# Splitting 32 weight units ahead of time: the attention's weights are split during the first MLP and parked in DRAM as two parts

## The chip, the cores and the metric

The kernel runs on one core of a Trainium2 chip, alone, as one program. The metric is the device time of that program in microseconds; several executions are timed and the median is given. The engines named here are TensorE (PE, with its weight loads PEld), VectorE (DVE), ScalarE (ACT), GpSimd (POOL) and SyncE (SP, which only issues DMAs). Line numbers such as L190 are lines of the kernel before; lines of the changed kernel are some 30 to 36 higher.

## The reference

A two-layer decoder trunk on 512 tokens of width 1024, with 16 learned meta tokens in front (528 columns in all), in float32:

```python
h = concat(meta, x)
# layer 0: mLSTM heads beside an RG-LRU branch, one output projection
h = h + ab_mixer(rmsnorm(h, norm_mix[0]))
h = h + mlp(rmsnorm(h, norm_mlp[0]), w1[0], w2[0])
# layer 1: differential attention, 8 heads, q/k of 2 x 64, v of 128, partial rotary
q, k, v = split(rmsnorm(h, norm_mix[1]) @ c_w_in)
p = softmax(q0 k0^T) - lam * softmax(q1 k1^T)      # causal, per head
h = h + (rmsnorm(p @ v) * subln * (1 - lambda_init)) @ c_w_out
h = h + mlp(rmsnorm(h, norm_mlp[1]), w1[1], w2[1])
out = rmsnorm(h, norm_final)[16:]
# mlp(x, w1, w2) = square(relu(x @ w1)) @ w2, hidden width 4096
```

## The kernel before

**Units.** All large weights lie in DRAM as 225 units `wu[u]` of 128 x 1024 float32 (512 KB). The list `seq` gives the order in which they are used: places 65 to 128 are the first MLP, 129 to 152 the attention's q, k and v projections (three units for each of 8 heads), 153 to 160 the attention's output projection, 161 to 224 the second MLP.

**Two parts.** A product in near float32 precision is made of three passes on rounded operands: each operand is split into a high part, rounded to the type `fp32r`, and a low part, the rest. `emit_load` does this for a unit: SP loads it into `raw` (two buffers), ACT casts it into `wh` (L159) and DVE subtracts, `wl = raw - wh` (L115, the helper `sub`). For the places listed in `POOL_L` the subtraction is done by POOL. `wh` and `wl` have three buffers each, so a part of unit i can be written only when the matmuls of unit i-3 are done. `get_w` sees to it that the load of unit i+2 is written down when unit i is used.

**A unit's matmuls.** `unit_mm` (L190) runs 8 blocks of the contraction times 3 passes, on 528 columns in two halves of 264 (48 matmuls) or on 512 columns (24 matmuls). Results lie in four PSUM buffers `mm`; a unit of two halves takes two of them, so PE can run one unit ahead of the engine that reads the results.

**The first MLP** (`mlp`) goes through four quarters `q`. In each, eight units give `a0` to `a7`: DVE scales and clips the PSUM result into `rt` (L662), ACT squares it (L664) and splits it, ACT the high and DVE the low part (`a7h`, `a7l`). Eight more units `c` multiply these and DVE adds the results onto `h` (L673). At the end `norm_x` turns `h` into the split operand `dx` of the next layer; the squares `nsq` are added up by POOL (L243) for the root-mean-square `drstd`.

**The attention.** `attend(hd)` runs the three projections of a head. The rotary part goes over ACT (`qr`), DVE (`qs`, a shuffle, then a product with the table `tb`), POOL (`qr * tb`), DVE (sum, split into `rh` and `rl`), and SP DMAs that lay the halves out as `st` and `kz`. In between stand the steps of the heads before (`slot`, `SLOTS`): scores `psc`, their maximum (DVE, L810), exponentials `e` (ACT, L817), the combination of the two softmaxes (DVE, L827), its transposes `pt` (PE, L838), the split `pp`, and the product `po`.

**Order.** The program is recorded in the order of the Python code and a scheduler of the framework then sets each engine's own order, by priorities (`soon()`, `pri()`) and by its own model of durations. On the chip each engine takes its instructions strictly in that order and waits in front of the first that is not ready; so an instruction that waits holds up all behind it on its engine.

Of the kernel before, what the change touches and what calls it, by code (L numbers as in the profile page):

```python
# [10 lines left out]
F32 = mybir.dt.float32  # L11
F32R = mybir.dt.float32r
# [4 lines left out]
P = 128  # L17
# [20 lines left out]
U_MLP0 = 65  # L38
# [14 lines left out]

POOL_OPS = "Mm"

POOL_L = {5, 33, 43, 44, 52, 126, 140, 143, 149, 151, 155, 159, 161, 164}
N_S = 31

N_KZ = 3
LOAD1 = 9  # L60
# [4 lines left out]
C_NMIX0, C_NMIX1, C_NMLP0, C_NMLP1, C_NFIN, C_MN, C_CW, C_CB, C_BR, C_BI, C_LAM, C_SUB, C_IB, C_FB = (  # L65
    0, 8, 16, 24, 32, 40, 48, 80, 88, 96, 104, 112, 113, 114)
# [3 lines left out]
def unit_of(t):  # L70
    a = [int(c) for c in t[1:]]
    if t[0] == "q":
        return U_HEAD + 6 * a[0] + a[1]
    if t[0] == "e":
        return U_GATE
    if t[0] == "o":
        return U_O + a[0]
    return U_LRU + 4 * (a[0] // 2) + a[0] % 2 + (2 if t[0] == "g" else 0)


def trunk(tc, hT, wu, wri, pk, lv, rope, gf, out, probe=None):
    nc = tc.nc
# [6 lines left out]
    with ctx:  # L89
        cp = ctx.enter_context(tc.tile_pool(name="cp", bufs=1))  # L90
        wr = ctx.enter_context(tc.tile_pool(name="wr", bufs=2))
        wp = ctx.enter_context(tc.tile_pool(name="wp", bufs=3))
# [3 lines left out]
        dr = ctx.enter_context(tc.tile_pool(name="dr", bufs=1, space=bass.MemoryType.DRAM))  # L96
# [7 lines left out]
        def sc(name, dt=F32, w=T):  # L104

            return big.tile([P, T], dt, tag="s", name=name, bufs=N_S)

# [6 lines left out]
        def sub(eng, o, a, b):  # L114
            eng.tensor_tensor(out=o, in0=a, in1=b, op=ALU.subtract)  # L115

        def split(hl, src, sl=slice(0, T), eng=None):
            nc.scalar.copy(hl[0][:, sl], src)  # L118
            sub(eng or nc.vector, hl[1][:, sl], src, hl[0][:, sl].bitcast(F32))
# [15 lines left out]
        def soon():  # L135
            return tc.high_priority(offset=BOOST)
# [4 lines left out]

        seq = list(range(N_UNIT))
        ready = []
        seq[0:U_OUT0] = [unit_of(t) for t in PLAN if t[0] in "qeocg"]
        seq[U_OUT0:U_OUT0 + 16] = [U_OUT0 + (8 + i) % 16 for i in range(16)]
        state = {"next": 0, "use": 0}

        def emit_load():
            i = state["next"]
            u = seq[i]  # L150
            raw = wr.tile([P, 1024], F32, tag="raw", name=f"raw{i}")
            nc.sync.dma_start(out=raw, in_=wu[u])
            if u >= N_UNIT - 8:
                wh, wl = (wp.tile([P, 1024], F32R, tag="wf" + p, name=f"w{p}{i}", bufs=8) for p in "hl")
            else:
                wh = wp.tile([P, 1024], F32R, tag="wh", name=f"wh{i}")
                wl = None if u == U_GATE else wp.tile([P, 1024], F32R, tag="wl", name=f"wl{i}")
            with soon():
                nc.scalar.copy(wh, raw)  # L159
                eng = nc.gpsimd if i in POOL_L else nc.vector  # L160
                if u == U_GATE:

                    hi, r = (a.rearrange("p (k c) -> p k c", k=KB) for a in (wh, raw))
                    sub(eng, hi[:, :, 64:100], r[:, :, 0:36], hi[:, :, 0:36].bitcast(F32))
                else:
                    sub(eng, wl, raw, wh.bitcast(F32))
            ready.append((wh, wl))
            state["next"] += 1

        def get_w(u):  # L170
            while state["next"] <= min(state["use"] + 2, len(seq) - 1):
                emit_load()
            assert seq[state["use"]] == u
            state["use"] += 1
            return ready.pop(0)
# [472 lines left out]
        dump("h1", h)  # L648


        def mlp(u0, gc, lo, tag, last=None):
            n = T - lo
            mx, terms = norm_x(h, gc, lo, tag)
            for q in range(4):
                a = []
                for j in range(KB):
                    ps = unit_mm(u0 + q * 16 + j, mx, lo, n)
                    if q == j == 0:
                        rs, _ = norm_r(terms, lo, tag)
                    t = sc("rt")  # L660
                    for p, tk in ps:
                        nc.vector.scalar_tensor_tensor(out=t[:, tk], in0=p, scalar=0.0, in1=rs[:, tk],  # L662
                                                       op0=ALU.max, op1=ALU.mult)
                    nc.scalar.activation(out=t[:, lo:], in_=t[:, lo:], func=AF.Square)  # L664
                    a.append(xt(f"a{j}"))
                    split(a[j], t[:, lo:], slice(lo, T))
                if q == 3 and last:
                    last(a)
                else:
                    for c in range(KB):  # L670
                        ps = unit_mm(u0 + q * 16 + 8 + c, a, lo, n)
                        for p, tk in ps:
                            nc.vector.tensor_tensor(out=h[:, c, tk], in0=p, in1=h[:, c, tk], op=ALU.add)  # L673

        mlp(U_MLP0, C_NMLP0, 0, "m")
        dump("h2", h)


# [209 lines left out]
        for part, ks in enumerate(OUT_K):  # L888
            w = None
            for i, (c, k) in enumerate((c, k) for c in range(KB) for k in ks):  # L890
                if i % 8 == 0:
                    w = get_w(U_OUT1 + (6 if part else 0) + i // 8)
# [165 lines left out]
```

## Time and profile before

| | before |
|---|---|
| median of 3 timed executions | 1478.97 us (1477.08 to 1480.21) |
| the profiled execution's own time | 1478.3 us |
| its span, first to last instruction | 1476.5 us |
| PE busy | 1448.5 us (98%) |
| DVE busy | 808.0 us (55%) |
| ACT busy | 646.3 us (44%) |
| POOL busy | 126.5 us (9%) |
| DMA | 142.97 MB, mean 97 GB/s |

The profiled execution's time is 1.8 us above its span, and 0.7 us below the median of the timed ones. Busy times are unions of an engine's instructions. Matmuls are pipelined, so that a busy PE is not a PE at its peak, but an idle PE is time lost.

### The profile page before, as it was taken

To read this page: it belongs to the slowest core of one execution; us is meant where nothing else is said; L and a number is where in the kernel's file an instruction comes from. 1 tells how busy PE (TensorE), PEld (TensorE's weight loads), DVE (VectorE), ACT (ScalarE), POOL (GpSimd) and SP (SyncE) were. 2 spreads that over 40 slices of the span, in tenths; PEclk is the share of its full clock that TensorE was granted. 3 is DMA by queue.
4 is the path that set the end of the run, shared out by engine and by line. 5 is a ranking of instruction groups with operands and counts; after the bars stand their busy time and mean duration, and the time that the engine had idled before them with its cause. 6 is when DMAs were issued, how large, how long until landed. Compare 5 with 4: busy or idle time off the path is not lost. (4 is left out here: it accounts for less than half of the span.)

```text
span 1476.5 us, 24167 instructions
## 1 busy us (share of the span) xinstructions
PE 1448.5 (98%) x9970; PEld 1344.5 (91%) x9970; DVE 808.0 (55%) x1385; ACT 646.3 (44%) x1122; POOL 126.5 (9%) x100
## 2 busy tenths in 40 slices
PE   8999999999999999999999999999999999999998
PEld 7999999999999999999999988888887888888886
DVE  6867745657544434334344588778765434343452
ACT  6454744747334313223134446666664223142342
POOL 4100001010011000000002211111132000000001
PEclk9999999999999999999999999999999999999999
DMA  7342323231232232232232354433222233233231
GB/s 255 96 115 79 100 72 121 72 100 46 85 100 87 86 97 91 86 98 89 87 100 87 107 138 109 110 87 105 83 73 86 88 98 101 87 99 99 87 125 46
DMA packets 50075, 142.97 MB, mean 97 GB/s; under 512 B 9482, under 2 KB 11031, under 8 KB 49964
## 3 DMA queue, kind: packets, MB, share of 16 engines
q1 hardware_dynamic: 49388, 140.37, 31.4%
q8 instruction: 78, 1.28, 0.4%
q10 hardware_dynamic: 576, 1.05, 0.2%
q14 instruction: 33, 0.27, 0.1%
HBM read 128.55 MB, written 2.16 MB: 89 GB/s over the span
## 5 line engine op out<-in xcount | busy, mean ns | idle before, releaser
L159 ACT CAST wh<-raw 128x1024 fp32r<-128x1024 f32 x225 | 236.1, 1050 | 614.7 <-PE mm L190 510.9
L115 DVE TENSOR_TENSOR wl<-raw,wh 128x1024 fp32r<-128x1024 f32 x210 | 261.2, 1244 | 78.9 <-ACT wh L159 78.2
L673 DVE TENSOR_TENSOR h<-mm,h 128x264 f32<-128x264 f32 (+1 forms) x88 | 41.3, 499 | 188.6 <-PE mm L190 188.6
L243 POOL TENSOR_TENSOR nsq<-nsq 128x528 f32<-128x528 f32 (+1 forms) x28 | 49.1, 1754 | 447.3 <-DVE wl L115 336.0
L662 DVE SCALAR_TENSOR_TENSOR rt<-mm,mrstd 128x264 f32<-128x264 f32 x64 | 24.7, 428 | 89.1 <-PE mm L190 89.1
L662 DVE SCALAR_TENSOR_TENSOR rt<-mm,nrstd 128x512 f32<-128x512 f32 x32 | 22.1, 692 | 80.2 <-PE mm L190 80.1
L115 POOL TENSOR_TENSOR wl<-raw,wh 128x1024 fp32r<-128x1024 f32 x14 | 33.4, 2388 | 216.2 <-ACT wh L159 171.3
L817 ACT ACTIVATE e<-psc,mx 128x264 f32<-128x264 f32 (+3 forms) x80 | 38.0, 479 | 10.9 <-DVE mx L810 7.1
L664 ACT ACTIVATE rt<-rt 128x528 f32<-128x528 f32 (+1 forms) x64 | 40.6, 636 | 2.8 <-DVE rt L662 2.8
L810 DVE TENSOR_REDUCE mx<-psc 128x1 f32<-128x264 f32 (+3 forms) x80 | 33.3, 429 | 14.2 <-PE psc L805 7.7
L749 POOL TENSOR_TENSOR qr<-qr,tb 128x512 f32<-128x512 f32 (+1 forms) x16 | 22.8, 1427 | 157.7 <-DVE qs L748 138.7
L946 POOL TENSOR_TENSOR zg<-z,gfr 128x512 f32<-128x512 f32 x4 | 5.2, 1300 | 343.8 <-DVE z L944 337.9
L633 DVE TENSOR_TENSOR h<-mm,h 128x264 f32<-128x264 f32 x32 | 12.4, 428 | 39.7 <-PE mm L190 39.7
L804 PE MATMUL psc<-st,st 128*128 128x264 f32 (+3 forms) x80 | 28.1, 352 | 4.1 <-ACT e L817 2.5
L190 PE MATMUL mm<-ax0h,wh 128*128 128x264 f32 x98 | 22.0, 298 | 6.2 <-ACT ax0h L232 6.2
L850 ACT CAST pp<-pt 128x128 fp32r<-128x128 f32 (+2 forms) x64 | 20.4, 342 | 16.8 <-PE pt L838 7.0
L804 PEld LDWEIGHTS psc<-st,st 128*128 128x128 f32 x80 | 15.2, 190 | 12.6 <-ACT e L817 6.5
L115 DVE TENSOR_TENSOR pp<-pt,pp 128x128 fp32r<-128x128 f32 (+2 forms) x64 | 23.8, 377 | 2.7 <-ACT pp L850 2.6
L118 ACT CAST rh<-qr 128x512 fp32r<-128x512 f32 (+1 forms) x16 | 10.0, 627 | 33.9 <-DVE qr L751 33.9
L805 PE MATMUL psc<-kz,st 128*128 128x264 f32 (+3 forms) x80 | 24.1, 302 | 0.3 <-DMA kz<-rl 0.2
L750 DVE TENSOR_TENSOR qs<-qs,tb 128x512 f32<-128x512 f32 (+1 forms) x16 | 23.1, 1446 | 0.0
L190 PE MATMUL mm<-a4h,wl 128*128 128x264 f32 (+1 forms) x88 | 22.6, 316 | 0.0
(799 smaller groups left out, 4786.8 us busy)
## 6 DMA issues: line engine op xcount, KB each, us to landing
raw<-wu SPq DMA_DIRECT2D x225, 512.0 KB
h<-hT SPq DMA_DIRECT2D x16, 264.0 KB
st<-rh SPq DMA_DIRECT2D x32, 132.0 KB
kz<-rl SPq DMA_DIRECT2D x16, 132.0 KB
st<-rh SPq DMA_DIRECT2D x16, 128.0 KB
st<-rl SPq DMA_DIRECT2D x16, 128.0 KB
cb<-crow SPq DMA_DIRECT2D x4, 264.0 KB
erb<-crow SPq DMA_DIRECT2D x4, 264.0 KB
```

Source lines behind the costliest of these rows:

```text
L115: eng.tensor_tensor(out=o, in0=a, in1=b, op=ALU.subtract)
L159: nc.scalar.copy(wh, raw)
L190: nc.tensor.matmul(p[:, :m], w[:, c], xx[:, s:s + m], start=(k == 0 and j == 0), stop=(k == KB - 1 and j == len(terms) - 1))
L243: nc.gpsimd.tensor_tensor(out=fin[0][:, lo:], in0=fin[0][:, lo:], in1=sq[:, lo:], op=ALU.add)
L662: nc.vector.scalar_tensor_tensor(out=t[:, tk], in0=p, scalar=0.0, in1=rs[:, tk], op0=ALU.max, op1=ALU.mult)
L664: nc.scalar.activation(out=t[:, lo:], in_=t[:, lo:], func=AF.Square)
L673: nc.vector.tensor_tensor(out=h[:, c, tk], in0=p, in1=h[:, c, tk], op=ALU.add)
L750: pool_or_dve("tT"[w]).tensor_tensor(out=sh[:, lo:], in0=sh[:, lo:], in1=tb[1][:, lo:], op=ALU.mult)
L804: nc.tensor.matmul(d[:, :m], qS[c][:, qs], kS[c][:, s0:s0 + m], start=True, stop=False)
L805: nc.tensor.matmul(d[:, :m], qS[c][:, qs], kL[c][:, s0:s0 + m], start=False, stop=s0 + m != nk)
L810: nc.vector.tensor_reduce(out=mx[:, 2 * c + r:2 * c + r + 1], in_=d[:, :m], axis=AX.X, op=ALU.max, negate=True)
L817: nc.scalar.activation(out=e[:, s0:s0 + m], in_=d[:, :m], func=AF.Exp, bias=mx[:, 2 * c:2 * c + 1], accum_out=ss[:, c + 2 * r:c + 2 * r + 1])
```

## The change

The 32 units of places 129 to 160 (`AHEAD`) no longer pass through `raw` and a split in the attention. Instead `make_ahead`, called after every second unit of the first MLP and twice behind it, does one step of a three-step pipeline each time: it writes the split halves of an earlier unit to DRAM (four DMAs of 256 KB), splits the unit that was loaded last (ACT and DVE, two halves of 128 x 512), and loads the next unit in two halves (two DMAs of 256 KB). All six DMAs of a step are issued by GpSimd. In the attention SP loads the two parts, 512 KB each, straight into `wh` and `wl`. Six places of `POOL_L` fall away with the splits that they named.

```diff
-POOL_L = {5, 33, 43, 44, 52, 126, 140, 143, 149, 151, 155, 159, 161, 164}
+POOL_L = {5, 33, 43, 44, 52, 126, 161, 164}
+AHEAD = range(129, 161)
+        parts = [[dr.tile([P, 1024], F32, name=f"part{i}{p}") for p in "hl"] for i in AHEAD]
 def emit_load():
             i = state["next"]
             u = seq[i]
+            if i in AHEAD:
+                wh, wl = (wp.tile([P, 1024], F32R, tag="w" + p, name=f"w{p}{i}") for p in "hl")
+                for w, part in zip((wh, wl), parts[i - AHEAD[0]]):
+                    nc.sync.dma_start(out=w.bitcast(F32), in_=part)
+                ready.append((wh, wl))
+                state["next"] += 1
+                return
+        def make_ahead():
+            while made:
+                part, t = made.pop(0)
+                nc.gpsimd.dma_start(out=part, in_=t[:, :512].bitcast(F32))
+            while came:
+                i, c, raw = came.pop(0)
+                hl = sc("rah", F32R), sc("ral", F32R)
+                split(hl, raw, slice(0, 512))
+                made.extend((part[:, c], t) for part, t in zip(parts[i - AHEAD[0]], hl))
+            if ahead:
+                i = ahead.pop(0)
+                for c in (slice(0, 512), slice(512, 1024)):
+                    raw = sc("ra")[:, :512]
+                    nc.gpsimd.dma_start(out=raw, in_=wu[seq[i]][:, c])
+                    came.append((i, c, raw))
 mlp: after each odd j, and after each odd c
+                    if between and j % 2:
+                        between()
+                        if between and c % 2:
+                            between()
-        mlp(U_MLP0, C_NMLP0, 0, "m")
+        mlp(U_MLP0, C_NMLP0, 0, "m", between=make_ahead)
+        make_ahead()
+        make_ahead()
```

The scheduler's order shows where the new instructions stand. The first place is the second half of the second quarter of the first MLP, on ACT: before, the casts of the weights stood there alone (number 92 belongs to the unit that is used three units later).

```order
L159 CAST wh92_7135<-raw92_7133 128x1024
L159 CAST wh93_7193<-raw93_7191 128x1024
L159 CAST wh94_7251<-raw94_7249 128x1024
L159 CAST wh95_7309<-raw95_7307 128x1024
L159 CAST wh96_7367<-raw96_7365 128x1024
```

On ACT, at the same place, of the changed kernel (`ra` is a loaded half of an attention unit, `rah` its high part):

```order
L169 CAST wh92_7375<-raw92_7373 128x1024
L120 CAST rah_7435<-ra_7311 128x512
L120 CAST rah_7439<-ra_7313 128x512
L169 CAST wh93_7449<-raw93_7447 128x1024
L120 CAST rah_7567<-ra_7443 128x512
L120 CAST rah_7571<-ra_7445 128x512
L169 CAST wh94_7507<-raw94_7505 128x1024
L120 CAST rah_7699<-ra_7575 128x512
L120 CAST rah_7703<-ra_7577 128x512
L169 CAST wh95_7581<-raw95_7579 128x1024
L120 CAST rah_7831<-ra_7707 128x512
L120 CAST rah_7835<-ra_7709 128x512
```

One whole step stands behind each of four weight casts in a row (the step of unit 140 first, that of 143 last), and none behind the next four. On POOL, which had nothing there before, the same steps of units 140 and 141 read so in the changed kernel:

```order
L187 DMA part140h_103<-rah_7435 128x512
L187 DMA part140h_103<-rah_7439 128x512
L197 DMA ra_7443<-wu 128x512
L197 DMA ra_7445<-wu 128x512
L187 DMA part140l_104<-ral_7436 128x512
L187 DMA part140l_104<-ral_7440 128x512
L187 DMA part141h_105<-rah_7567 128x512
L187 DMA part141h_105<-rah_7571 128x512
L197 DMA ra_7575<-wu 128x512
L197 DMA ra_7577<-wu 128x512
```

The loads of a step stand behind the stores of the high parts of the step before it. The second place is the attention, on DVE, where one head's scores and the next head's rotary part meet. Before:

```order
L748 STREAM_SHUFFLE qs<-qr 128x512
L810 TENSOR_REDUCE mx<-psc 128x1
L750 TENSOR_TENSOR qs<-qs,tb_9547 128x512
L824 RECIPROCAL rs_11532<-ss 128x2
L115 TENSOR_TENSOR pp<-pt,pp 128x2x128
L751 TENSOR_TENSOR qr<-qr,qs 128x512
L825 TENSOR_TENSOR rs_11532<-rs_11532,lam 128x1
L824 RECIPROCAL rs_11589<-ss 128x2
L115 TENSOR_TENSOR pp<-pt,pp 72x2x128
L825 TENSOR_TENSOR rs_11589<-rs_11589,lam 128x1
L115 TENSOR_TENSOR rl<-qr,rh 128x512
L827 SCALAR_TENSOR_TENSOR e_11508<-e_11508,rs_11532,e_11521 128x528
```

On DVE, the same stretch of the changed kernel:

```order
L117 TENSOR_TENSOR pp<-pt,pp 128x2x128
L860 RECIPROCAL rs_12068<-ss 128x2
L117 TENSOR_TENSOR pp<-pt,pp 72x2x128
L861 TENSOR_TENSOR rs_12068<-rs_12068,lam 128x1
L860 RECIPROCAL rs_12125<-ss 128x2
L861 TENSOR_TENSOR rs_12125<-rs_12125,lam 128x1
L117 TENSOR_TENSOR pp<-pt,pp 128x128
L863 SCALAR_TENSOR_TENSOR e_12044<-e_12044,rs_12068,e_12057 128x528
L863 SCALAR_TENSOR_TENSOR e_12112<-e_12112,rs_12125,e_12119 128x144
L784 STREAM_SHUFFLE qs<-qr 128x512
L846 TENSOR_REDUCE mx<-psc 128x1
L786 TENSOR_TENSOR qs<-qs,tb_10119 128x512
```

The combination `e` (L827, now L863) stands ahead of the shuffle and the table product instead of behind them. The third place is SP's queue around the k projection of head 3 (unit 139). Before:

```order
L152 DMA raw_11095<-wu 128x1024
L152 DMA raw_11238<-wu 128x1024
L764 DMA st_10916<-rh 64x512
L765 DMA st_10916<-rl 64x512
L764 DMA st_10917<-rh 64x512
L765 DMA st_10917<-rl 64x512
L152 DMA raw_11320<-wu 128x1024
L764 DMA st_11047<-rh 64x528
```

And on SP in the changed kernel:

```order
L157 DMA wh_11064<-part140h 128x1024
L157 DMA wl_11065<-part140l 128x1024
L157 DMA wh_11144<-part141h 128x1024
L157 DMA wl_11145<-part141l 128x1024
L800 DMA st_11104<-rh 64x512
L800 DMA st_11105<-rh 64x512
L801 DMA st_11104<-rl 64x512
L801 DMA st_11105<-rl 64x512
L157 DMA wh_11281<-part142h 128x1024
L157 DMA wl_11282<-part142l 128x1024
L800 DMA st_11233<-rh 64x528
```

Each weight load became two of the same size, at the same places between the rotary DMAs.

## Rows read from the trace of the kernel before

**Rows 1.** The page's head: span, and each engine's busy time with its share of the span and its number of instructions.

```profile
span 1476.5 us, 24167 instructions
PE 1448.5 (98%) x9970; PEld 1344.5 (91%) x9970; DVE 808.0 (55%) x1385; ACT 646.3 (44%) x1122; POOL 126.5 (9%) x100
```

**Rows 2.** Windows: the first 37 us; most of the first MLP; the attention up to its last output units; the passage to the second MLP; 50 us of the second MLP (matmuls of 512 columns). [...]

```profile
0.00:37.00 37.00, 30.13 (x225) 29.41 (x226) 22.33 (x35) 23.89 (x38) 17.08 (x20) 1.00 0.72 254
480.00:805.00 325.00, 325.00 (x2688) 325.00 (x2687) 134.19 (x199) 96.55 (x121) 5.97 (x3) 1.00 0.30 91
830.00:1092.00 262.00, 253.42 (x1607) 222.01 (x1606) 200.83 (x452) 159.07 (x404) 38.91 (x23) 0.99 0.37 100
1092.00:1117.00 25.00, 22.12 (x88) 17.30 (x87) 17.78 (x19) 14.86 (x23) 17.20 (x9) 0.93 0.27 84
1150.00:1200.00 50.00, 50.00 (x217) 40.51 (x217) 18.45 (x21) 11.68 (x14) 0.00 (x0) 1.00 0.32 95
```

**Rows 3.** What PE waited for from 830 to 1092 us: who waited, on whom; us in total, times, longest.

```profile
PE pt L838 <- DVE e L827: 3.2, 5, 0.7
PE psc L804 <- ACT e L817: 2.5, 4, 1.5
PE psc L804 <- DVE v1l L115: 1.3, 2, 0.7
...
PE psc L805 <- DMA kz<-rl: 0.2, 1, 0.2
```

**Rows 4.** The instructions that read or write `raw`, in the same stretch: busy time and number on DVE (the subtractions), ACT (the casts) and POOL (the subtractions of `POOL_L`), clock, DMA share, GB/s.

```profile
830.00:1092.00 262.00, 30.44 (x24) 30.37 (x29) 14.27 (x6) 0.99 0.37 100
```

**Rows 5.** Timeline of DVE around one of the waits of `pt` for `e` (start, length, instruction), then PE's row that waited.

```profile
939.21 1.55 DVE L750 TENSOR_TENSOR qs<-qs,tb 128x512 f32<-128x512 f32 x1
...
942.45 0.69 DVE L115 TENSOR_TENSOR rl<-qr,rh 128x512 fp32r<-128x512 f32 x1 [0.16 <-ACT rh L118]
943.09 1.04 DVE L827 SCALAR_TENSOR_TENSOR e<-e,rs,e 128x528 f32<-128x528 f32 x2
...
943.91 0.74 PE L838 MATMUL pt<-ident,e 128*72 128x128 f32 x5 [0.75 <-DVE e L827]
```

**Rows 6.** The longest wait of that stretch: ACT's timeline, PE's row that waited, and the windows of the wait and of the 3.4 us after it (columns as in rows 2).

```profile
963.03 1.04 ACT L159 CAST wh<-raw 128x1024 fp32r<-128x1024 f32 x1
963.98 0.62 ACT L118 CAST co2h<-rqy 128x512 fp32r<-128x512 f32 x1
964.50 0.48 ACT L817 ACTIVATE e<-psc,mx 128x264 f32<-128x264 f32 x1
...
965.12 0.34 PE L804 MATMUL psc<-st,st 128*128 128x144 f32 x1 [1.46 <-ACT e L817]
...
963.00:965.10 2.10, 0.66 (x4) 0.41 (x3) 2.00 (x6) 2.10 (x6) 0.00 (x0) 1.00 0.00 0
966.80:970.20 3.40, 3.40 (x16) 3.39 (x15) 3.25 (x10) 1.12 (x4) 1.08 (x1) 0.50 0.38 148
```

**Rows 7.** ACT's timeline ahead of one of the two waits for `v1l`.

```profile
925.35 1.05 ACT L159 CAST wh<-raw 128x1024 fp32r<-128x1024 f32 x1 [1.04 <-PE mm L190]
926.31 0.59 ACT L867 ACTIVATE osq<-po 128x512 f32<-128x512 f32 x1
926.79 0.52 ACT L789 CAST v1h<-pv 72x256 fp32r<-72x256 f32 x2
```

**Rows 8.** Durations (ns, smallest, median, largest) of a cast and a subtraction of 128 x 512 or 528 in the attention, and POOL's product on the same shape.

```profile
L118 ACT CAST rh<-qr x16: 620/628/636, 846.0 to 1040.6; 128x512 fp32r<-128x512 f32 x8, 128x528 fp32r<-128x528 f32 x8
L115 DVE TENSOR_TENSOR rl<-qr,rh x16: 677/700/710, 846.7 to 1041.3; 128x512 fp32r<-128x512 f32 x8, 128x528 fp32r<-128x528 f32 x8
L749 POOL TENSOR_TENSOR qr<-qr,tb 128x512 f32<-128x512 f32 (+1 forms) x16 | 22.8, 1427 | 157.7 <-DVE qs L748 138.7 <-DVE tb L746 9.9 <-DVE rs L825 9.1
```

**Rows 9.** SP's issue of one weight load in the first MLP (ns, smallest, median, largest), and windows behind the issue at 638.52 us (columns as in rows 2).

```profile
L152 SPq DMA_DIRECT2D raw<-wu x55: 327/328/328, 481.6 to 795.3; - x55
638.52 0.33 SPq L152 DMA_DIRECT2D raw<-wu  x1
639.50:640.50 1.00, 1.00 (x11) 1.00 (x10) 0.00 (x0) 0.00 (x0) 0.00 (x0) 1.00 0.77 221
640.50:641.50 1.00, 1.00 (x11) 1.00 (x10) 0.00 (x0) 0.00 (x0) 0.00 (x0) 1.00 0.73 295
```

**Rows 10.** The end of a first half (`a7`) in the first MLP, on ACT and DVE, with the first result of the second half.

```profile
595.25 1.06 ACT L159 CAST wh<-raw 128x1024 fp32r<-128x1024 f32 x1 [3.38 <-PE mm L190]
...
596.34 1.23 DVE L115 TENSOR_TENSOR wl<-raw,wh 128x1024 fp32r<-128x1024 f32 x1
597.77 0.71 DVE L115 TENSOR_TENSOR a7l<-rt,a7h 128x528 fp32r<-128x528 f32 x1 [0.20 <-ACT a7h L118]
601.18 0.77 DVE L673 TENSOR_TENSOR h<-mm,h 128x264 f32<-128x264 f32 x2 [2.71 <-PE mm L190]
```

**Rows 11.** From the first MLP to the attention: POOL's last sum of squares and its first rotary product, and on DVE a weight subtraction in front of head 0's rotary part.

```profile
830.20 1.80 POOL L243 TENSOR_TENSOR nsq<-nsq 128x528 f32<-128x528 f32 x1 [4.00 <-ACT nsq L241]
841.89 1.62 POOL L749 TENSOR_TENSOR qr<-qr,tb 128x512 f32<-128x512 f32 x1 [9.89 <-DVE tb L746]
...
842.28 2.32 DVE L115 TENSOR_TENSOR wl<-raw,wh 128x1024 fp32r<-128x1024 f32 x1
844.52 0.68 DVE L750 TENSOR_TENSOR qs<-qs,tb 128x512 f32<-128x512 f32 x1
```

More of the change, by code (lines that the diff above doesn't have):

```diff
@@ L168, in emit_load @@
             state["next"] += 1
+        ahead = list(AHEAD)
+        came, made = [], []
+        def make_ahead():
[13 more added lines that the diff above has]
+                    came.append((i, c, raw))
         def get_w(u):
@@ L648, in trunk, with mlp @@
         dump("h1", h)
-        def mlp(u0, gc, lo, tag, last=None):
+        def mlp(u0, gc, lo, tag, last=None, between=None):
             n = T - lo
```

## The prediction

> **What bounds the kernel now.** I read the page's head first: PE is busy for 1448.5 of 1476.5 us [rows 1], so a change can win little more than what PE idles, and only where it idles. The windows show where. In the first MLP PE is busy for all of 325.00 us, while DVE works 134 and ACT 97 of them [rows 2]: those two have room, PE has none. In the attention from 830 to 1092 us PE idles 262.00 - 253.42 = 8.6 us, and there DVE is busy for 201 and ACT for 159 of 262 us [rows 2]. PE's waits say for what [rows 3]: five times `pt` waits for DVE's `e` (3.2 us), four times `psc` for ACT's `e` (2.5 us), twice for `v1l` (1.3 us); a DMA is waited for once, 0.2 us. The work on weights in that stretch, 30.4 us on DVE, 30.4 on ACT and 14.3 on POOL [rows 4], is what the change takes away. It is mostly hidden: PE idles 8.6 us in all.
>
> The longest of these waits costs more than its length. [...] The most that the attention can give back is therefore 8.6 + 1.7 = 10.3 us. The waits behind 1092 us, where the clock is 0.93 in the mean [rows 2], stand at the second MLP's own weights and its norm, which the change leaves alone.
>
> **What goes.** (1) The five waits for `e`. In the case shown, `e` stood behind a table product of 1.55 us and a subtraction of 0.69, and PE waited 0.75 [rows 5]. The order of the changed kernel puts `e` ahead of both, some 2 us earlier: I take all 3.2 us. What is late next is the rotary part, behind two `e` of 1.04 us together; nothing there waits for it but the `kz` DMAs. (2) The waits for ACT's `e`: in the longest a weight cast of 1.04 us stood right in front of the chain [rows 6]; without it 0.4 us is left and the clock, I suppose, stays up. I take 1.0 us there and 0.4 of the three smaller ones, 1.4 us, and the clock's 1.7. (3) Before `v1l` a cast of 1.05 us stood two places ahead [rows 7]: 0.8 of the 1.3 us. Sum: 3.2 + 1.4 + 1.7 + 0.8 = 7.1 us; bounds 0, if the waits only move, and 10.3.
>
> **What the attention pays.** Each unit brings a second 512 KB. SP issues one in 0.33 us, and the bytes move in about two windows of 1 us, at 221 and 295 GB/s [rows 9]. The stretch's DMA share of 0.37 at 100 GB/s [rows 2] grows by 29 casts' worth of bytes (30.4 us of them at 1.05 each [rows 4, 7]), 15 MB on 26, to about 0.6. A load may start when unit i-3 is done and is needed two units later, 11 us or more (24 matmuls of 50 / 217 = 0.23 us each are 5.5 us [rows 2]); two parts need 0.33 + 2 x 2 + 1, some 5 us: hidden. Not surely hidden are the `st` and `kz` DMAs, which now find up to 1 MB in front of them. From nothing to 2 us for each of 8 heads; I take the 0.2 us that one head waits today [rows 3] for each, 1.6 us.
>
> **What the first MLP pays.** 64 casts of 0.63 us are 40 us on ACT, and 64 subtractions of 0.70 are 45 us on DVE [rows 8]: ACT comes to 137 and DVE to 179 of 325 us, both below PE. The cover is PE's own pace: 2688 matmuls are 56 units of 48, 5.80 us each [rows 2]. What can break it is lateness, since ACT and DVE stop at a `rah` or `ral` whose data has not landed, and weights and `h` sums stand behind. The order spreads steps two units apart in the first half of a quarter, but in the second half four steps stand one unit apart (five in the last quarter). Call t the time that GpSimd needs to issue one DMA. No row shows it. Below it is SP's 0.33 us for rows of the same number [rows 9], above it POOL's sum of 1.80 [rows 11], which touches every element; I take 0.9, midway between SP's issue and POOL's product of 1.43 on the same shape [rows 8].
>
> A step's cycle is the largest of 6t (its DMAs); 3t + 3.5 (a store, two loads, 2.9 us to landing as at 638.5, a cast); and its bytes, 1.57 MB and a weight unit's 0.52, at 300 GB/s (91 at a share of 0.30 [rows 2]), 6.9 us. That gives 6.9 us against 5.8. The slack: counted from the end of the first half (595.2), DVE is done with `wl` and one half subtraction at +3.1 [rows 10]; a store, two loads, landing, cast and subtraction follow, to 7.0 + 3t. The `h` sum behind belongs to the unit that ends at +11.6 and must start by 17.4 - 0.8 = 16.6, or PE finds no PSUM buffer. So 9.6 - 3t = 6.9 us of slack at first, of which three more steps use 3 x 1.1 = 3.3. PE does not wait: 0 us. The `a7` chain, 598.5 against its use at about 600.2, moves by one cast or subtraction of 0.7 and holds.
>
> At the passage POOL's seven sums stand behind the last stores: five steps of 1.1 us late, two more issues, and then 1.8 us each, they end about 2 us later than at 832.0 [rows 11]. The subtraction of 2.32 us ahead of head 0's `qs` [rows 11] is gone: 0 us net, 2 us if that cover fails.
>
> **Sum.** -7.1 + 1.6 = -5.5 us on the profiled execution's 1478.3, which stands 0.7 us below the median of the runs shown, 1478.97: 1473.5 us.
>
> [...] Beside POOL's product at 841.9 DVE's subtraction took 2.32 us [rows 11] instead of 1.23 [rows 10], 1.9 times. If issuing suffered alike from DVE, t = 0.9 x 1.9 = 1.7, the cycle is 10.2, three steps overrun the slack of 4.5 by 8.7 us in each quarter, and the time is 1473.5 + 35 = 1508 us; a part of the first rival's chance is this. [...]
>
> [...]
>
> **Rivals.**
> - *GpSimd issues too slowly (17%, slower).* The place is the second half of each quarter. The point of decision is 3 x (6t - 5.8) = 9.6 - 3t, t = 1.3 us. At 1.43 PE loses 8.3 - 5.3 = 3.0 us per quarter, 12 in all: 1485.5. At 1.80 it is 15 - 4.2 = 10.8, 43 in all: 1516.5. For it: POOL needs 1.4 to 1.8 us for anything of this size. Against: issuing touches 128 rows, not 65536 elements.
> - *The waits only move (22%, no change).* DVE still works 170 of 262 us in the attention, and the rotary part now stands behind `e`. With a new wait of 0.5 to 1 us per head, 4 to 8 us, the gain of 5.5 is gone: 1477 to 1481, middle 1478.5. For it: 75 us of work removed covers only 8.6 us of idle PE. Against: the waits named in rows 5 to 7 have the removed work, or a changed order, in them.
> - *Weights in front of `st` and `kz` (11%, slower).* 1 us per head instead of 0.2 gives 1480, 2 us gives 1488. For it: SP's queue is in order and each load became two. Against: one DMA wait of 0.2 us today.
>
> **How the numbers follow.** Likeliest (50%): 1473.5, its own range 1469 to 1476 (all of the 10.3 us at one end, half of the gain at the other). What a measurement can tell from no change is about 0.2%, 3.0 us, so 1476.0 to 1481.9. Faster 0.50 from the first case; same 0.23, from the moved waits and the mildest of the queue's case; slower 0.27, from the rest. The range of 1468 to 1488 takes in the moved waits, the queue's case and the mild end of slow issuing; left out is most of the slow issuing, some 12%, and a few per cent below.
>
> **What would show it.** PE without waits from 480 to 805 us, and fewer than 3 us of them from 830 to 1092, with no stretch at half clock near its middle; POOL's issues of about 0.9 us. Waits of `pt` for `e` gone confirm (1). PE waiting in the second halves of the first MLP for `h` or weights, with ACT idle in front of `rah` on a DMA, means slow issuing; PE waiting for `kz` or `st`, or for `wh` or `wl` on a DMA, means the queue. Wrong would be, above all, the price of an issue.

## The result, and the profile after

The changed kernel takes 1464.36 us (median of 4, 1463.24 to 1466.47) against 1478.03 us of the kernel before (median of 4): a ratio of 0.9910, 95% interval 0.9888 to 0.9931. That is 13.7 us faster, where 5.5 were forecast, and below the forecast range of 1468 to 1488 us. The profiled execution took 1463.2 us. The page's head, answering to [rows 1]:

```profile
span 1461.4 us, 24650 instructions
PE 1437.9 (98%) x9970; PEld 1338.6 (92%) x9970; DVE 814.5 (56%) x1423; ACT 650.8 (45%) x1154; POOL 214.0 (15%) x286
```

The same 9970 matmuls keep PE busy for 10.6 us less than before. The windows of the changed kernel, which answer to [rows 2] (columns there and here: stretch, its length, busy time and number of instructions of PE, PEld, DVE, ACT and POOL, granted clock of PE as a share of its full one, mean busy share of the 16 DMA engines, GB/s):

```profile
480.00:805.00 325.00, 325.00 (x2691) 325.00 (x2690) 165.13 (x255) 125.90 (x175) 96.40 (x176) 1.00 0.71 230
805.00:830.00 25.00, 25.00 (x194) 24.32 (x194) 14.68 (x24) 11.34 (x20) 15.42 (x21) 1.00 0.94 330
830.00:1092.00 262.00, 258.03 (x1658) 228.57 (x1657) 182.67 (x442) 141.94 (x390) 35.92 (x23) 1.00 0.53 167
1092.00:1117.00 25.00, 22.16 (x95) 17.50 (x94) 15.90 (x16) 13.10 (x20) 9.63 (x6) 1.00 0.26 72
```

In the first MLP PE is busy for all of 325.00 us, as before, with 31 us more work on DVE and 29 on ACT beside it. In the attention it idles 4.0 us instead of 8.6. What PE still waits for from 830 to 1092 us, answering to [rows 3] (who, on whom: us, times, longest):

```profile
PE pt L874 <- DVE e L863: 2.1, 3, 1.1
PE psc L840 <- ACT e L853: 0.9, 4, 0.2
PE nps L282 <- POOL nsq L273: 0.4, 1, 0.4
PE psc L840 <- DVE pp L117: 0.2, 1, 0.2
```

L117, L120, L169 and L220 of the changed kernel are L115, L118, L159 and L190 of the kernel before. No wait for a DMA is left, and none for `v1l`. To see where the 15 us between the two profiles went, take the same work out of both, from the first matmul of head 1's first projection to that of the second MLP's first unit. Before:

```profile
847.00:1115.50 268.50, 257.41 (x1572) 222.56 (x1573) 209.31 (x459) 165.24 (x413) 51.18 (x30) 0.99 0.37 100
```

After:

```profile
846.10:1101.40 255.30, 248.92 (x1575) 219.00 (x1573) 181.63 (x435) 139.09 (x384) 38.08 (x23) 1.00 0.52 160
```

13.2 us of the 15.1 are here. Idle time fell from 11.09 to 6.38, by 4.7 us; busy time fell by 8.5 us. Of these, some 2.7 are half clock that the changed kernel's profile doesn't have: 1.7 us lost in the 3.4 us of [rows 6], and 1.0 in the first 1.9 us of another such stretch, which begins at 1113.6 (below). The last 5.8 us are matmuls that kept PE busy for longer before, at full clock. Some groups of PE in that stretch (line, operation, form, count, then busy us and mean ns of one, then idle); before:

```profile
L804 PE MATMUL psc<-st,st 128*128 128x400 f32 x16 | 6.8, 426 | 0.8 <-ACT e L817 0.7
L862 PE MATMUL po<-pp,v1h 128*128 128x384 f32 x16 | 5.6, 382 | 0.0
L862 PE MATMUL po<-pp,v1h 72*128 72x512 f32 x32 | 11.1, 420 | 0.3
```

After:

```profile
L840 PE MATMUL psc<-st,st 128*128 128x400 f32 x16 | 6.2, 389 | 0.2 <-DVE pp L117 0.2
L898 PE MATMUL po<-pp,v1h 128*128 128x384 f32 x16 | 4.1, 339 | 0.0
L898 PE MATMUL po<-pp,v1h 72*128 72x512 f32 x32 | 10.4, 401 | 0.1
```

`po` of 384 columns was busy for 1.5 us less without any idle time in front of it, before or after. Counted from each start to the next start, its 16 rows gave back 0.7 us (3.53 against 2.84): before, matmuls of other groups stood between its own, and then a group's busy time contains the ends of rows that otherwise overlap. Of the 16 `psc`, two lay in the half clock of [rows 6]. PE's timeline before shows how a wait hides (start, length, instruction, idle in front):

```profile
933.59 0.40 PE L190 MATMUL mm<-dx6h,wl 128*128 128x512 f32 x1
933.82 0.40 PE L190 MATMUL mm<-dx7h,wh 128*128 128x512 f32 x1
934.06 0.24 PE L804 MATMUL psc<-st,st 128*128 128x144 f32 x1
...
934.35 0.44 PE L190 MATMUL mm<-dx7l,wh 128*128 128x512 f32 x1
934.70 0.34 PE L804 MATMUL psc<-st,st 128*128 128x144 f32 x1
...
935.65 0.40 PE L190 MATMUL mm<-dx0h,wh 128*128 128x264 f32 x2
935.89 0.41 PE L190 MATMUL mm<-dx0l,wh 128*128 128x264 f32 x2
936.86 0.45 PE L804 MATMUL psc<-st,st 128*128 128x400 f32 x1 [0.56 <-ACT e L817]
```

A matmul of 512 columns is followed 0.23 us later by the next, while its own row is 0.40 long: rows overlap. At 934.35 the next start comes after 0.35 us, 0.12 more than that, and no idle time is shown; for what, the trace doesn't say. At 935.89 two matmuls of 264 columns should take 0.24 and the next start comes after 0.97: lost are 0.73 us, shown 0.56. So the idle time of this page understates what a wait costs, here by 0.17 us, and leaves the 0.12 us out altogether.

An estimate over all starts of the stretch, the same 1572 matmuls in both profiles: set each against the spacing that the fastest third of its pairs (its form and that of the next) reaches. Then the waits with idle time shown fell by 6 to 7 us, not 4.7; lateness without idle time fell by some 3.7, half clock by some 2.4; and up to 1 us is that other pairs follow one another, since the scheduler gave PE another order after the change.

### The profile page after: what moved, and what is told of

It reads as the page before. It is cut to its first block, busy times and chain, and to the rows that moved or that the text cites. A ratio compares the mean times of both kernels' runs of the same rounds, so it can differ in the third digit from the quotient of the medians.

```text
span 1461.4 us, 24650 instructions
## 1 busy us (share of the span) xinstructions
PE 1437.9 (98%) x9970; PEld 1338.6 (92%) x9970; DVE 814.5 (56%) x1423; ACT 650.8 (45%) x1154; POOL 214.0 (15%) x286
## 5 line engine op out<-in xcount | busy, mean ns | idle before, releaser
L169 ACT CAST wh<-raw 128x1024 fp32r<-128x1024 f32 x193 | 202.6, 1050 | 503.7 <-PE mm L220 402.8
L117 DVE TENSOR_TENSOR wl<-raw,wh 128x1024 fp32r<-128x1024 f32 x184 | 227.1, 1235 | 66.9 <-ACT wh L169 66.5
L117 DVE TENSOR_TENSOR ral<-ra,rah 128x512 fp32r<-128x512 f32 x64 | 43.7, 688 | 56.4 <-ACT rah L120 56.4
L120 ACT CAST rah<-ra 128x512 fp32r<-128x512 f32 x64 | 39.5, 617 | 69.3 <-DMA ra<-wu 69.1
L117 POOL TENSOR_TENSOR wl<-raw,wh 128x1024 fp32r<-128x1024 f32 x8 | 19.2, 2403 | 201.6 <-ACT wh L169 120.4
L197 POOL DMA_DIRECT2D ra<-wu x64 | 34.7, 547 | 2.9 <-issue 2.9
L120 ACT CAST rh<-qr 128x512 fp32r<-128x512 f32 (+1 forms) x16 | 10.0, 627 | 51.2 <-DVE qr L787 48.2
L365 POOL TENSOR_SCALAR_AFFINE_SELECT cb<-cb 128x128 f32<-128x128 f32 (+2 forms) x20 | 7.7, 397 | 166.3 <-DMA cb<-crow 166.1
L886 ACT CAST pp<-pt 128x128 fp32r<-128x128 f32 (+2 forms) x64 | 21.0, 342 | 16.4 <-PE pt L874 14.4
L220 PE MATMUL mm<-ax0h,wh 128*128 128x264 f32 x98 | 22.0, 297 | 6.3 <-ACT ax0h L262 6.3
L117 DVE TENSOR_TENSOR pp<-pt,pp 128x128 fp32r<-128x128 f32 (+2 forms) x64 | 23.8, 382 | 3.6 <-ACT pp L886 3.5
```

Source lines behind the costliest of these rows:

```text
L197: nc.gpsimd.dma_start(out=raw, in_=wu[seq[i]][:, c])
L220: nc.tensor.matmul(p[:, :m], w[:, c], xx[:, s:s + m], start=(k == 0 and j == 0), stop=(k == KB - 1 and j == len(terms) - 1))
```

## The experiments

Each runs beside the kernel before on the same chip. Differences are of medians to that one's (1476.9 to 1478.0 us), so to set beside the -13.7 of the change; ratios carry the 95% interval.

### The gain without its price

```diff
-                for w, part in zip((wh, wl), parts[i - AHEAD[0]]):
+                for w, part in zip((wh, wl), parts[0]):
-        ahead = list(AHEAD)
+        ahead = list(AHEAD)[:1]
```

> The gain without its price: only unit 129 is split during the first MLP, and all 32 units of the attention load that unit's two parts (so the splits of 31 units are left out; the loads of the attention stay 2 x 512 KB per unit, and every engine's order in the attention stays that of the changed kernel). Theory A, the 31 splits and their 186 DMAs cost PE nothing in the first MLP: the time of the changed kernel, 1464.4, within 2 us. Rival B, the first MLP or the passage behind it pays a hidden 2 us or more: 1462 or less.

Measured 1463.52 us, -14.0, ratio 0.9908 (0.9895 to 0.9922). The first MLP's splits cost what can't be measured here. PE's order in the attention is that of the changed kernel but for 1%.

### The price without the gain

The changed kernel with `if False:` in place of `if i in AHEAD:` in `emit_load` and the old `POOL_L`.

```diff
-            if i in AHEAD:
+            if False:
```

> The price without the gain: the first MLP splits and stores all 32 units as in the changed kernel, but nobody reads the parts; the attention loads and splits its weights as before. Theory A: the time of before, 1478.0, within 2 us, and PE starts the attention's first matmul at 847 us as before. Rival B: 1480 or more.

Measured 1478.37 us, +0.9, ratio 1.0008 (1.0000 to 1.0017). At most a small price; in its profile PE waits at the passage to the attention for low parts, where the attention's own splits and the last of the ahead ones meet. The waits of PE from 826 to 845 us:

```profile
PE mm L220 <- DVE dx7l L263: 2.0, 1, 2.0
PE mm L220 <- ACT dx7h L262: 0.7, 1, 0.7
PE mm L220 <- DVE dx6l L263: 0.3, 1, 0.3
```

The changed kernel has none of these three.

### Only the casts, only the subtractions

`casts_gone` loads `wh` from the part and subtracts as before; `subs_gone` loads `wl` from the part and casts as before.

```diff
 # casts_gone
-                for w, part in zip((wh, wl), parts[i - AHEAD[0]]):
-                    nc.sync.dma_start(out=w.bitcast(F32), in_=part)
+                raw = wr.tile([P, 1024], F32, tag="raw", name=f"raw{i}")
+                nc.sync.dma_start(out=wh.bitcast(F32), in_=parts[i - AHEAD[0]][0])
+                nc.sync.dma_start(out=raw, in_=wu[u])
+                with soon():
+                    sub(nc.gpsimd if i in POOL_L else nc.vector, wl, raw, wh.bitcast(F32))
 # subs_gone, instead
+                nc.sync.dma_start(out=raw, in_=wu[u])
+                nc.sync.dma_start(out=wl.bitcast(F32), in_=parts[i - AHEAD[0]][1])
+                with soon():
+                    nc.scalar.copy(wh, raw)
```

> Half of the gain: in the attention the high part comes from DRAM, the low part is still made by a subtraction (DVE, or POOL at the six places of the old list), from a second load of the unit. So ACT loses 30 us of work, DVE none. If the gain comes from ACT (PE's waits for exponentials, and gaps too short to show as idle in front of scores): 1465 to 1469. If it comes from DVE (the waits of pt for e): 1474 to 1478. If it is the load on both together: about 1471.

> The other half: in the attention the low part comes from DRAM, the high part is still cast by ACT from a load of the unit. DVE and POOL lose their 45 us of subtractions, ACT none, and the order on DVE has e ahead of the table product, as in the changed kernel. If the gain comes from DVE: 1465 to 1469. If it comes from ACT: 1474 to 1478. If it is the load on both together: about 1471.

`subs_gone` took 1468.81 us, -8.7, ratio 0.9942 (0.9930 to 0.9954): putting back the casts alone costs 5.0 us of the 13.7. That is the slow end of what was expected if the gain came from DVE. `casts_gone` took 1498.25 us, +20.7, ratio 1.0137 (1.0120 to 1.0153), against all three expectations. Its DVE, in the attention, in the subtractions' group (busy us, mean ns, then idle in front and what ended it):

```profile
L117 DVE TENSOR_TENSOR wl<-raw,wh 128x1024 fp32r<-128x1024 f32 x24 | 29.3, 1222 | 26.9 <-DMA wh<-part146h 4.5 <-issue 4.1 <-DMA wh<-part152h 3.8
```

DVE stood 26.9 us in front of subtractions, mostly for the part's load. That load can start only when PE leaves the buffer `wh` (in `casts_gone` SP stood 24.1 us for that, nine times); before, the load went early into `raw`. And the kernel before has a smaller standing of the same kind, a row that the prediction didn't read:

```profile
L115 DVE TENSOR_TENSOR wl<-raw,wh 128x1024 fp32r<-128x1024 f32 x24 | 31.5, 1314 | 13.4 <-ACT wh L159 13.2
```

So the subtractions cost DVE 31.5 us of work and 13.4 of standing, and what stood behind them was late by both. The next runs try to part the two.

### Work, or standing

`casts_gone2` is `casts_gone` without `soon()`; `idle_subs` and `idle_subs2` are the changed kernel with subtractions of loaded parts into a scratch tile; `before_late` is the kernel before without `soon()` at these places; `work_only` has subtractions that touch no weight.

```diff
 # before_late
-            with soon():
+            with (nullcontext() if 129 <= i < 161 else soon()):
                 nc.scalar.copy(wh, raw)
 # idle_subs, in get_w, for the places of AHEAD (idle_subs2: without soon(), on the unit before)
+                raw = wr.tile([P, 1024], F32, tag="raw", name=f"raw{i}")
+                with soon():
+                    sub(nc.gpsimd if i in (140, 143, 149, 151, 155, 159) else nc.vector, raw, w[0].bitcast(F32), w[1].bitcast(F32))
 # work_only, after the split of each rotary part, and after vr
+        def extra(a, b):
+            r = wr.tile([P, 1024], F32, tag="raw", name="extra")
+            for c in range(2):
+                sub(nc.vector, r[:, 512 * c:512 * c + 512], a, b)
```

> The changed kernel with the attention's subtractions put back as mere load: when a unit comes into use, DVE (POOL at the six old places) subtracts its two parts, which landed long ago, into a scratch tile that nobody reads. No cast comes back, and no engine stops for a load. If the subtractions' work is what costs, it gives back what leaving them out gained: from 1464.4 to 1471 to 1475. If the gain of leaving them out came from the stops for loads and not from the work: 1464 to 1467.

> casts_gone with its subtractions put in line without priority, so that DVE should come to them after the high part has landed. If the 20 us that casts_gone lost came from DVE standing in front of loads: below 1478, and if the casts are worth the 4.4 us that separate subs_gone from the changed kernel, about 1473. If the loss came from the third load per unit (1.5 MB instead of 1.0): 1490 or more again.

> idle_subs without priority, and with the parts of the unit before, which PE is already using: the 25 subtractions of DVE and 6 of POOL are there as work, and DVE should not stand in front of a load. If the work is what costs: 1470 to 1475, about what leaving the subtractions out gained (8.7 us). If only the standing costs: 1464 to 1467.

> The kernel before, but the casts and subtractions of the places 129 to 160 are put in line without priority, in the order of the code: the same work as before, moved back a little, so that DVE and ACT should stand less often in front of a weight split (in the profile of before DVE idles 13.2 us in 14 stops in front of wl, waiting for ACT's cast, which waits for PE to leave wh). If this standing is a large part of what the change took away: 1470 to 1475. If it is the work itself: 1477 to 1479.

> The changed kernel with mere work put back on DVE: after each projection of a head two subtractions of 128 x 512 on tiles that are already there (rh and rl, or vr) into a scratch tile that nobody reads, 48 of 0.70 us, 33.6 us in all, about what the weight subtractions of before came to (30.4 us on DVE). None of them can stand in front of a weight's load or of ACT's cast. If the work is what costs: 1469 to 1475. If what costs is standing in front of weights (for the cast or the load): 1464 to 1467.

`idle_subs` took 1509.50 us (+31.5, ratio 1.0214, 1.0197 to 1.0231), `idle_subs2` 1499.63 (+22.7, 1.0150, 1.0132 to 1.0168), `casts_gone2` 1487.87 (+11.0, 1.0076, 1.0062 to 1.0089): all three worse than the kernel before, and none without standing, so what was expected of them doesn't hold. The subtractions came so early in DVE's order that on the chip DVE waited for the loads. The group in `idle_subs2`, and then in `casts_gone2`:

```profile
L117 DVE TENSOR_TENSOR raw<-wh,wl 128x1024 f32<-128x1024 f32 x24 | 32.6, 1359 | 11.2 <-DMA wl<-part149l 4.1 <-DMA wl<-part140l 3.0 <-DMA wl<-part146l 1.6
```

```profile
L117 DVE TENSOR_TENSOR wl<-raw,wh 128x1024 fp32r<-128x1024 f32 x26 | 31.7, 1217 | 21.4 <-issue 4.1 <-DMA wh<-part160h 3.4 <-DMA wh<-part152h 3.0
```

In `idle_subs2` this standing is no longer than the 13.4 us of the kernel before, so it doesn't explain the 22.7 us, and why that run is slow stays open. In `casts_gone` and `casts_gone2`, which stood for 26.9 and 21.4 us, the standing is a likely cause: two loads into `wh` and `wl` at the moment PE leaves them do no harm in the changed kernel, where no engine but PE, a unit or more later, reads them, and PE waits for no DMA from 830 to 1092 us. `before_late` took 1476.42 us (-0.5, ratio 0.9995, 0.9986 to 1.0003), but its DVE still stood 12.1 us in front of `wl`, so it says nothing on either:

```profile
L115 DVE TENSOR_TENSOR wl<-raw,wh 128x1024 fp32r<-128x1024 f32 x24 | 31.5, 1312 | 12.1 <-ACT wh L159 12.0
```

`work_only` comes nearest to parting them. Its 48 subtractions took 0.68 us each and stood for 0.3 us in all:

```profile
L117 DVE TENSOR_TENSOR extra<-rh,rl 128x512 f32<-128x512 f32 x32 | 20.8, 684 | 0.3
L117 DVE TENSOR_TENSOR extra<-vr 128x512 f32<-128x512 f32 x16 | 10.7, 676 | 0.0
```

It took 1470.11 us, -7.6, ratio 0.9953 (0.9939 to 0.9967). Mere work on DVE, in no one's way but by its place in line, gives back 6.1 of the 13.7 us. With the 5.0 of the casts that makes 11.1; the other 2.6 would be the standing and POOL's 14.3 us [rows 4], if such parts add up, which no run tells.

One rival is left in all of these runs. The scheduler makes a new order for each of them, for PE too: of the some 1570 matmuls of the attention about six in ten stand in the same sequence in `work_only` and `subs_gone` as in the changed kernel, and half in the kernel before. No run takes work away and holds the order, so how much of each difference is the order isn't shown. `gain_only`, `sp_issue` and `shift4` keep PE's order but for 1%, so this rival doesn't touch them.

### The order on DVE

```diff
-PRI = "EORSdn"
+PRI = "EORSdnN"
```

in the kernel before (`order_only`) and in the changed one (`after_n`).

> The kernel before with one letter added to PRI, so that the combination e goes to DVE with priority and stands ahead of the table product; no work is removed. If the order is what helps (term 1 of the prediction): the waits of pt for e, 3.2 us shown, go, and the time is 1474 or less. If the removed work is what helps: 1476 to 1479, with the waits moved to others.

> The changed kernel with the same letter added to PRI. If the three waits of pt for e that are left (2.1 us) come from e standing late in DVE's order: 1461 to 1463. If they come from the work in front of e being late itself: 1464, no change against the changed kernel.

Measured 1475.99 us, -1.2, ratio 0.9993 (0.9984 to 1.0002), and 1466.45 us, -10.8, ratio 0.9923 (0.9910 to 0.9937). The order alone does next to nothing: with `e` ahead of the table product, `pt` waits for the split `pp` instead, 3.3 us in place of the 3.2 of [rows 3]. PE's waits of `order_only`:

```profile
PE pt L838 <- DVE pp L115: 3.3, 5, 1.0
PE psc L804 <- DVE v1l L115: 2.0, 3, 1.2
```

`after_n` meets neither expectation: it is slower than the changed kernel, and there too the waits moved from `e` (2.1 us, then 0.3) to `pp` (2.1).

### Half of the units

```diff
-POOL_L = {5, 33, 43, 44, 52, 126, 161, 164}
+POOL_L = {5, 33, 43, 44, 52, 126, 140, 161, 164}
-AHEAD = range(129, 161)
+AHEAD = range(141, 161)
```

> AHEAD reduced to the places 141 to 160: heads 0 to 3 load and split their 12 units as before, heads 4 to 7 and the output projection are as in the changed kernel. If the gain grows with the number of units taken away: about 1471. If it sits at one place (the 1.46 us gap with the half clock behind it, head 4 on): 1465 to 1467.

Measured 1468.09 us, -9.9, ratio 0.9932 (0.9920 to 0.9945), between the two expectations: four heads' projections and the output's eight units give 72% of the gain, the other four heads the rest. It does not sit at one place.

### Who issues, and how much of it

`sp_issue` replaces `nc.gpsimd.dma_start` by `nc.sync.dma_start` in `make_ahead`; `issue_x4` keeps GpSimd and cuts each transfer into four.

```diff
 # issue_x4 (the loads likewise)
-                nc.gpsimd.dma_start(out=part, in_=t[:, :512].bitcast(F32))
+                for k in range(0, 512, 128):
+                    nc.gpsimd.dma_start(out=part[:, k:k + 128], in_=t[:, k:k + 128].bitcast(F32))
```

> The changed kernel with the loads and stores of the first MLP issued by SP instead of GpSimd. SP's queue is in order, and a store there waits for its subtraction, with the first MLP's own weight loads behind it. Theory: a queue of its own is what makes the price nothing, so here the first MLP's weights come late, PE waits between 480 and 830 us, and the time is 1468 to 1490. Rival: the weights have enough time (11 us and more between load and use), and it is 1464 as with GpSimd.

> The changed kernel with each of GpSimd's loads and stores cut into four of 128 x 128: 768 DMAs instead of 192, the same bytes. By the arithmetic of the prediction with the 0.55 us that an issue took in the changed kernel: a step is 24 issues, 13.1 us, against a unit of 5.8; three steps come 22 us late, the slack of 9.6 - 12 x 0.55 = 3.0 is overrun by 19 us in each quarter, 1464 + 76 = 1540 us. If a smaller DMA issues in less time, or the slack is larger than worked out: nearer to 1464.

`sp_issue`: 1462.80 us, -14.4, ratio 0.9898 (0.9882 to 0.9914). The theory falls: PE never waits from 480 to 830 us, though SP's queue did stand. SP's waits there:

```profile
SPq L187 <- ACT rah L120: 85.7, 24, 4.7
SPq L187 <- DVE ral L117: 5.5, 12, 1.1
```

A unit's load has 11 us and more, and stops of at most 4.7 don't use them up. `issue_x4`: 1547.43 us, +69.4, ratio 1.0459 (1.0438 to 1.0481). An issue takes the same for a quarter of the bytes (ns, smallest, median, largest), so a step is 13 us of issuing:

```profile
L199 POOL DMA_DIRECT2D ra<-wu x256: 537/537/747, 458.8 to 875.0; - x128
```

PE waits at the start of the second halves, where the first rival put the loss, but for the first halves' results and not for `h` or weights; ACT stands in front of `rah` on a load, 165.6 us in 41 stops, behind which those results stand in line. From 480 to 880 us:

```profile
PE mm L222 <- ACT a7h L120: 24.2, 3, 8.2
PE mm L222 <- ACT a6h L120: 5.5, 3, 1.9
PE mm L222 <- ACT a5h L120: 3.1, 2, 1.7
```

The rival's place is right, and its size is too large: the first quarter loses nothing, and the attention's first matmul starts 46 us later than in the changed kernel (873.3 against 826.9), where 76 were worked out. The other 37 us come behind it, where DVE waits 24.2 us at head 0's `qs` for a late store, among others. That the total comes near the 1540 expected is luck.

### A version that beats both

In the changed kernel's profile two waits of PE are left at the passage to the second MLP, 2.1 us for `nx6l` and 0.7 for `nx7l`. DVE's timeline there:

```profile
1093.28 1.19 DVE L263 SCALAR_TENSOR_TENSOR nx5l<-h,pkt,nx5h 128x512 fp32r<-128x512 f32 x1
1094.40 2.33 DVE L117 TENSOR_TENSOR wl<-raw,wh 128x1024 fp32r<-128x1024 f32 x1
1096.66 1.74 DVE L263 SCALAR_TENSOR_TENSOR nx6l<-h,pkt,nx6h 128x512 fp32r<-128x512 f32 x1
```

A split of the second MLP's own weights stands right in front of `nx6l`. `shift4` takes the second MLP's first four units ahead instead of the output projection's last four (with `parts[AHEAD.index(i)]` for the places), and `sp_shift4` also lets SP issue.

```diff
-AHEAD = range(129, 161)
+AHEAD = [*range(129, 157), *range(161, 165)]
-POOL_L = {5, 33, 43, 44, 52, 126, 161, 164}
+POOL_L = {5, 33, 43, 44, 52, 126, 155, 159}
```

> The changed kernel with the places 161 to 164 (the second MLP's first units) split ahead instead of 157 to 160 (the last of the attention's output projection). At the passage to the second MLP PE waits 2.8 us for the low parts nx6l and nx7l on DVE. If weight splits in front of them are part of that wait: 1462 to 1463.5. If not: 1464 to 1466, since four splits are back at the end of the attention.

> Both edits that were no slower, together: SP issues the loads and stores of the first MLP, and the places 161 to 164 stand in for 157 to 160. If they add up: 1457 to 1459.5. If SP's queue, which now also carries these stores into the passage to the attention, delays something: 1460 or more.

`shift4`: 1459.86 us, -17.4, ratio 0.9880 (0.9866 to 0.9893); `sp_shift4`: 1459.94 us, -18.1, ratio 0.9876 (0.9863 to 0.9890). Both beat the change by some 4 us, `shift4` by more than expected; who issues makes no difference that can be measured, so the two edits don't add up. In `shift4` PE idles 0.4 us in that stretch instead of 2.8, which is 2.4 of the 4 us; the rest isn't traced. In windows as above:

```profile
1092.00:1117.00 25.00, 24.62 (x108) 19.71 (x107) 13.72 (x16) 13.08 (x20) 5.02 (x4) 1.00 0.36 127
```

## Why the prediction was wrong, point by point

**What the first MLP pays: 0 us, right.** PE is busy for 325.00 of 325.00 us. The unknown price t is 0.54 us, below the 0.9 taken. The changed kernel's loads (ns, smallest, median, largest; then us to landing):

```profile
L197 POOL DMA_DIRECT2D ra<-wu x64: 541/543/748, 458.3 to 814.3; - x64
DMA to landing us min/median/max: 3.0/5.0/6.3
```

Landing took 5.0 us instead of the 2.9 assumed, and ACT did stop at `rah` for 69.1 us in 21 places; the slack held both. `a7l` was done at 597.85 instead of 598.5. The slowing by 1.9 that the prediction worked out for issuing beside DVE, to 1.7 us each and 1508 us in all, doesn't show here: 45 of these 64 issues had a subtraction of DVE beside them for a part of their time or all of it, 19 had none, and both have a median of 543 ns; the largest is 748.

**The passage: 0 us net, right.** POOL's seven sums ended at 833.4 instead of 832.0, and head 0's `qs` started at 841.3 instead of 844.5 [rows 11]; PE waited 0.4 us for `nsq`.

**What the attention pays: 1.6 us forecast, none found.** No wait for `st`, `kz` or a part is left; the DMA share rose to 0.53 in place of 0.37, near the 0.6 worked out.

**What goes: 7.1 us forecast; this is the step that failed, and with it the ceiling of 10.3 us.** It rests on the prediction's first step, that a change can win little more than what PE idles, and only where it idles. The stretch above gave back 13.2 us. The named waits behaved about as said in sum, if not one by one: `pt` for `e` kept 2.1 of 3.2 us, where all was to go; `psc` for ACT's `e` fell from 2.5 to 0.9, `v1l` from 1.3 to nothing, and the clock's 1.7 us came. Shown idle time fell by 4.6 us in the attention, against 5.4 forecast. What the sum left out is the 5.8 us inside PE's busy time, which a ceiling made of idle time can't hold, and half clocks elsewhere. The reason given for (1) was wrong too: the order of `e` on DVE alone brings next to nothing (`order_only`, 1.2 us), while work that comes back costs 6.1 (`work_only`) and 5.0 us (`subs_gone`). That it is the work by itself, and not the order that the scheduler makes with it, isn't shown.

**The half clock.** The prediction counted one stretch: the 1.7 us in its sum and in its ceiling are half of the 3.40 us that [rows 6] shows at a granted clock of 0.50, behind the gap of 1.46 us. The profile before has three ahead of the kernel's end, the changed one none. Two of them follow gaps that are still there: one at 361 us (2.24 us idle, then 2.22) and one at the passage to the second MLP. Before, windows of that passage:

```profile
1109.00:1111.00 2.00, 0.49 (x3) 0.05 (x1) 2.00 (x2) 0.00 (x0) 2.00 (x1) 1.00 0.14 16
1111.00:1113.00 2.00, 0.96 (x3) 0.49 (x3) 2.00 (x2) 0.00 (x0) 1.65 (x2) 1.00 0.81 246
1113.60:1117.00 3.40, 3.40 (x9) 2.67 (x9) 0.00 (x0) 2.39 (x4) 1.85 (x1) 0.50 0.00 0
```

After, the same place:

```profile
1096.00:1098.00 2.00, 0.34 (x2) 0.00 (x0) 2.00 (x2) 0.00 (x0) 1.92 (x2) 1.00 0.36 47
1098.00:1100.00 2.00, 0.96 (x3) 0.49 (x3) 2.00 (x2) 0.00 (x0) 1.53 (x1) 1.00 0.57 215
1100.50:1103.90 3.40, 3.40 (x17) 2.83 (x16) 0.00 (x0) 3.15 (x5) 2.06 (x1) 1.00 0.00 0
```

PE idles as long, and once 9 matmuls follow in 3.4 us, once 17. In `gain_only`, with the same gap, the half clock is there again (0.93 in the mean from 1092 to 1117 us, against 1.00 here). So this part of the difference between two profiles is chance; in the medians it is at most a part, since the executions of the changed kernel vary by it too (1463.24 to 1466.47). Executions of like mean granted clock tell its share roughly: the kernel before took 1475.6 us at 0.998 and 1476.9 at 0.997 (last section), the changed one 1463.34 and 1465.37 at 0.998 and 1466.47 at 0.997. They lie 10 to 12 us apart, so 1 to 4 of the 13.7 go with the clock, on few executions; without them the gain is still about twice the forecast.

**The rivals.** That the waits only move was wrong in sum, but `order_only` does just that. Slow issuing doesn't apply at 0.54 us; its price for the first MLP was too high (`issue_x4`: 46 us where its arithmetic gives 76). Weights in front of `st` and `kz` didn't happen.

## What to carry to other kernels

The ceiling of a gain on the engine that bounds is not its idle time (10.3 us was the ceiling here, 13.2 came back): measure from start to start of its instructions, against the spacing that the same form has in an undisturbed row, and put a short wait at its whole length. A group's busy time also grows when other instructions come between its own (`po` of 384 columns: 1.5 us, of which 0.7 are left from start to start), so it is no measure of lateness either. Before costing work that leaves an engine, read also how long that engine stood in front of it (13.4 us here); and let a load that starts late be read only by the engine that needs it last (in `casts_gone` DVE read such loads too, and stood 26.9 us). A price that hides behind the bound engine can be checked in one run by taking the gain away, and its margin by multiplying the price.

## What the runs showed of the hardware

- GpSimd's issue of a DMA took 0.54 us for 256 KB and for 64 KB alike, of 128 rows each; SP's took 0.33 us for 512 KB [rows 9] and 0.42 in the median for 256 KB (`sp_issue`): it is a price per DMA here, not per byte.
- Which engine issues made no difference to the whole that can be measured here: 1464.4 us with GpSimd and 1462.8 with SP, and 1459.9 with either in `shift4` and `sp_shift4`.
- A gap of PE of the same length (2.24 and 2.22 us, at 361 us) was followed by half clock in one execution and not in another. Of 64 executions of the kernel before, those with a mean granted clock of 0.998 took 1475.6 us in the median, with 0.997 1476.9, with 0.996 and 0.995 1478.2, with 0.994 1479.7: most of this kernel's spread goes with the clock.
